# One hybrid decoder layer on Trainium2: tokens laid out by remainder modulo 4 within each tile of 128

## The chip, the cores and the metric

The kernel runs on one core of one Trainium2 chip. The metric is the device time of one launch in microseconds (us). A core has five engines, each with its own queue of instructions that it works through in order: TensorE (PE; PEld is its loading of weights), VectorE (DVE), ScalarE (ACT), GpSimd (POOL) and SyncE (SP), which here issues all transfers. Sixteen DMA engines carry them.

## The reference

One decoder layer over x of 1 x 1024 x 1024 (tokens x channels), float32:

```python
z = x @ w_in
u, rq, rk, rv, rg, aq, ak, av = split(z)
y_ssm = rms_norm(s5_mixer(u, ...), ssm_norm)        # 256 channels, state space model
y_ret = retention_mixer(rq, rk, rv, rg, ret_norm)   # 4 heads of 64, chunks of 128
y_att = rms_norm(dilated_attention_mixer(aq, ak, av), attn_norm)  # 8 heads of 64
h = concatenate([y_ssm, y_ret, y_att]) @ w_out
x = layer_norm(ALPHA * x + h, ln1_w, ln1_b)
h = square(relu(x @ mlp_w1)) @ mlp_w2
x = layer_norm(ALPHA * x + h, ln2_w, ln2_b)
```

The attention has three branches with (window, dilation) of (128, 1), (512, 4) and (2048, 16); a query of the second looks at keys 0, 4, 8, ... tokens back, so queries and keys fall into four classes by the token's remainder modulo 4.

## The kernel before

Products are done in pieces: an operand is split into a rounded part and a rest ("hi" and "lo", `H` and `L` in names), and three matmuls stand for one. Tokens are worked on in 8 tiles of 128 and in blocks of 512. A planner written in Python orders the work: the class `Clock` has a cost for each operation, transfers too, `Stream` starts coroutines by rank and blocks them at `when` and `flag`, and the order so found is the order of each engine's queue. On the chip the queues run in order, and what waits in one holds up all behind it.

The stages, in order of time: the projection by w_in (`dense`, its jobs' results taken from PSUM by `ev_u` and others); the state space model (`ssm_params`, `ssm`), retention, attention; the output projection in three parts (`out_b` with g = 0 and 1, `out_a`); layer norm 1; the MLP as products of sums of blocks (`up_sums`, `product`, `down`), layer norm 2 (`norm2`). The first are interleaved with one another.

The pieces that the change and the prediction speak of (all operations but matmuls and transposes are recorded with line 234, matmuls with line 394, transposes with 400):

- `ev_u` (L619): the part u of the projection, `uf`, is copied from PSUM by ScalarE in four pieces, and stored to `u_d` in DRAM in sixteen transfers, each `8x16x128` in the DRAM access pattern. `Tz` (L921) is loaded from `ker_d` by two transfers with an access pattern of 8 x 16 x 1024 on the DRAM side and 128 partitions on the other.
- `ssm` (L930): the gate, `og`, is the product of `glth` and `gT` on VectorE; then squares, scale and store to `mix_d`.
- `values` (L1218): V goes to DRAM (`v_d`) and comes back with its rows grouped in fours (`w`).
- `far` (L1251): scores of the near branch (y = 0) and the dilated branches (y = 1) of a head, 16 matmuls of 128x256 per head, `ps_f`; Q and K are read every fourth element for y = 1, and for y = 0 Q is cast once to an order by remainder, `by_r`.
- `mixed` (L1469): the sum of the hi and lo parts of the attention output, `mixp`, on VectorE.
- `load_x1` (L1616): once the last job of the projection is done ("last"), x is loaded into `X`, one transfer of 512 KB for each of the 8 token tiles; `out_b` for g = 0 adds products to them (`X<-X,pm`, in `add_b`, L1624).
- `out_b_load` and `out_b_split` (L1571, L1586) load W_out and the mix in pieces of 512 KB (`wraw`), cast them on ScalarE (`MB`) and find the rest on GpSimd; `out_b` for g = 1 has the matmuls `pm<-MB`.
- `down` (L2072): `rraw` is the MLP's inner result, read back from `r_d` in 512 KB pieces; `norm2` (L2045) stores the output `out` by `put`, a whole tile or parts of it, as the layer norm of a tile is done. The stores stand among the loads of `rraw` in SyncE's queue.

Of the kernel before, what the change touches and what calls it, by code (L numbers as in the profile page):

```python
# [13 lines left out]
F32R = mybir.dt.float32r  # L14
# [52 lines left out]
RET_LG = [math.log(1.0 - 2.0 ** (-5.0 - h)) for h in range(4)]  # L67


def shape_tables():  # L70

    qi = np.arange(128)[:, None]
    x = np.arange(512)[None, :]
    near = lambda d: (d <= 128).astype(np.float64)
    far = lambda d: ((d % 4 == 0) & (d <= 512)).astype(np.float64) + (d % 16 == 0)
    parts = []
    by_r = 4 * (qi % 32) + qi // 32
    for d, mult in ((384 + qi - x, lambda d: near(d) + far(d)), (128 + by_r - x[:, :256], near),
                    (4 * (128 + qi - x[:, :256]), far)):
        n = mult(d) * (d >= 0)  # L80
        lnc = np.log(np.where(n > 0, n, 1.0))
        parts.append(np.stack([np.where(n > 0, 2.0 ** -(h + 1.0) * d - lnc, 1e30) for h in range(NH)]))
    bias = np.concatenate(parts, 2)
    i = np.arange(128)
    df = i[None, :] - i[:, None]
    dm = np.stack([np.where(df >= 0, np.exp(np.maximum(df, 0) * lg), 0.0) for lg in RET_LG])
    dmat = dm.reshape(2, 2, 128, 128).transpose(2, 1, 0, 3)
    zeta = np.concatenate([np.repeat(np.exp((127.0 - i) * lg)[:, None], 64, 1) for lg in RET_LG], 1)
    xi = np.stack([np.concatenate([np.repeat(np.exp((i + 1.0) * RET_LG[2 * p + e])[None], 64, 0)
                                   for e in range(2)]) for p in range(2)], 1)  # L90
    f = lambda a: np.ascontiguousarray(a, dtype=np.float32)
    tabs = np.concatenate([zeta, xi.reshape(128, 256), dmat.reshape(128, 512)], 1)
    return {"c_bias": f(bias), "c_tabs": f(tabs)}
# [204 lines left out]
async def when(w, early=0.0):  # L298
    if isinstance(w, str):
        await ask(("flag", w))  # L300
    elif w:
        await ask(("data", w, early))
# [3 lines left out]
def trunk_kernel(ctx: ExitStack, tc: tile.TileContext, t_in, out):  # L306
# [43 lines left out]
    def free(*tiles):  # L350

        for t in tiles:
            if isinstance(t, (list, tuple)):
                free(*t)
            else:
                room = st_.room[tags.pop(t.tensor.name)]
                room[0] += 1
                room[1].append(clock.last[t.tensor.name])

    def U(shape, dt=F32, name="u", spare=2):  # L360
        return take(up, shape, dt, "u", NU, name, spare)

    async def Us(n, shape, dt=F32, name="u", spare=2):
        return [await U(shape, dt, name, spare) for _ in range(n)]
# [13 lines left out]
    def f(ap):  # L378
        return ap.bitcast(F32)
# [4 lines left out]
    async def stt(o, a, s, b, op0, op1):  # L384
        await dve.scalar_tensor_tensor(out=o, in0=a, scalar=s, in1=b, op0=op0, op1=op1)
# [233 lines left out]
    def ev_u(a):  # L619

        async def g(th, ps):
            if th == 0:
                T["uf", a] = await U([128, 8, 128], name="uf", spare=0)
            uf = T["uf", a]
            await act.copy(uf.rearrange("p j c -> p c j")[:, 64 * th:64 * th + 64], ps.rearrange("p (c j) -> p c j", j=8))
            free(ps)
            if th == 1:
                for j in range(8):
                    d = u_d[a][112 - 16 * j:128 - 16 * j]
                    await sp.dma_start(out=bass.AP(tensor=d.tensor, offset=d.offset, ap=[[128, 8], [1024, 16], [1, 128]]),  # L630
                                       in_=uf[:, j])
                free(T.pop(("uf", a)))
                T["UT", a] = await U([128, 8, 128], name="UT", spare=0)
                await sp.dma_start(out=T["UT", a], in_=u_d[a].rearrange("p (g c) -> p g c", g=8))
        return g
# [294 lines left out]
    async def ssm():  # L930
# [100 lines left out]
        for a in range(2):  # L1031
# [5 lines left out]
                await act.copy(gT[a][:, 4 * jq:4 * jq + 4], ps)  # L1037
                free(ps)
            free(gel[a])
        og = await Us(2, [128, 128, 8], name="og", spare=0)  # L1040
        sq = await Us(2, [128, S], name="sq", spare=0)
        jc = lambda v: v.rearrange("p j c -> p (j c)")
        for fo in range(2):
            for jq in range(2):
                q = slice(4 * jq, 4 * jq + 4)
                await when([gT[0][:, q], gT[1][:, q], wg])
                ps = await PS(name="ps_gl")
                for k in range(2):
                    await mm(ps, wg[:, k, fo * 128:(fo + 1) * 128], jc(gT[k][:, q]), k == 0, k == 1)
                th = await H([128, 4, 128], name="glth")  # L1050
                await act.activation(jc(th), ps, AF.Tanh, scale=0.25, bias=bglu[:, fo:fo + 1])
                await when([th])
                free(ps)
                await stt(og[fo].rearrange("p c j -> p j c")[:, q], th, 1.0, gT[fo][:, q], A_, M)
                free(th)
        free(wg, gT)
        for fo in range(2):
            o = og[fo].rearrange("p c j -> p (c j)")
            await when([o])
            await act.activation(sq[fo], o, AF.Square, scale=0.25)  # L1060
            await dve.tensor_scalar_mul(o, o, ssmw[:, fo:fo + 1])
            await sp.dma_start(out=mix_d[fo], in_=o)
            free(og[fo])
# [154 lines left out]
    async def values(p):  # L1218
# [18 lines left out]
        flag(f"V{p}")  # L1237
        for a in range(2):
            W = await U([128, 4, 2, 2, 64], F32R, "w")
            await sp.dma_start(out=f(W).rearrange("p r h s d -> p (r h s d)"),  # L1240
                               in_=v_d[p][512 * a:512 * a + 512].rearrange("(c r) v -> c (r v)", r=4))
            T["W", p].append(W)
        flag(f"W{p}")

# [6 lines left out]
    async def far(i_, h):  # L1251
# [7 lines left out]
            flag(f"stat{p}")  # L1259
        await when(f"stat{p}")  # L1260
        stat = T["stat", p]
        by_r = await U([128, 4, 4, 32], F32R, "by_r")
        await act.copy(by_r, Qs[:, 512:].rearrange("p (s a r) -> p s r a", s=4, r=4))
        P = await Us(2, [128, 4, 256], name="far")
        for y in (1, 0):
            s = P[y]
            for j in range(0, 4, 2):
                await when([Qs, KL, KH, bias] if y else [by_r])
                ps = await PS((128, 2, 256), "ps_f")
                qk = []  # L1270
                for a in (j, j + 1):
                    q = Qs[:, 512 + a:S:4] if y else by_r[:, a].rearrange("p r a -> p (r a)")
                    qk.append((q, slice(384 + 128 * a, 640 + 128 * a) if y == 0 else slice(a, S, 4)))
                for i, (q, k) in enumerate(qk):
                    await mm(ps[:, i], q, KH[:, k], i == 0, False)
                for i, (q, k) in enumerate(qk):
                    await mm(ps[:, i], q, KL[:, k], False, i == 1)
                for i in range(2):
                    await dve.tensor_tensor_reduce(
                        out=s[:, j + i], in0=ps[:, i], in1=bias[:, 512 + 256 * y:768 + 256 * y], scale=1.0,  # L1280
                        scalar=3e38, op0=ALU.add, op1=ALU.min, accum_out=stat[:, y, j + i, e, 0:1])
                free(ps)
        scored(h)
        free(by_r)
        for y in (1, 0):
            for j in range(4):
                await act.activation(P[y][:, j], P[y][:, j], AF.Exp, scale=-1.0, bias=stat[:, y, j, e, 0:1],
# [181 lines left out]
    async def mixed(h, po, c0, n, ms, classes=1):  # L1469
# [7 lines left out]
        mix = T["mix", p]  # L1477
        vl = await H([64, n], name="vl")
        await act.copy(vl, po[64:128, :n])
        by_r = lambda v: v.rearrange("p (r a) -> p r a", r=classes)  # L1480
        await tt(dve, mix[b, c].rearrange("p (a r) -> p r a", r=classes), by_r(po[:64, :n]), by_r(vl), A_)
        free(vl, po)
        if not counted(("mix", p, c0), 2):
            return
# [111 lines left out]
    async def out_b(g):  # L1596
# [16 lines left out]
        else:  # L1613
            flag("outb")

    async def load_x1():  # L1616
        await when("last")
        X1 = big("A", [128, 8, D], "X1", F32)
        x1.extend(X1[:, t] for t in range(8))
        for t in range(8):  # L1620
            await sp.dma_start(out=x1[t], in_=x_d[t * 128:(t + 1) * 128, :])
            flag(f"xl{t}")

    async def add_b(t, dh, g, ps, v):  # L1624
# [219 lines left out]
    async def up_sums():  # L1844
        for q in range(NQ):
            await when(f"ul{q}")
            wa, wb = raws["u", q]
            s1 = await U([128, 2, 512], name="ws", spare=3)
            s3 = await U([128, 2, 512], name="ws", spare=3)
            raws["us", q] = s1, s3  # L1850
            await tt(dve, s1[:, 0], wb[:, 0], wb[:, 1], A_)
            await tt(dve, s1[:, 1], s1[:, 0], wa[:, 0], SUB)
            await tt(dve, s3[:, 0], wa[:, 0], wb[:, 0], SUB)
            await tt(dve, s3[:, 1], wa[:, 1], s1[:, 1], SUB)
            flag(f"us{q}")
# [188 lines left out]

    async def norm2(t):  # L2045
        def put(c):
            return sp.dma_start(out=out_d[t * 128:(t + 1) * 128, c], in_=x1[t][:, c])

        await when("ln2")
        await layer_norm(t, lnw["ln2_w"], lnw["ln2_b"], put)  # L2050
# [84 lines left out]
def host_arrays(inputs):  # L2135

    src = {n: np.ascontiguousarray(inputs[n]) for n in _INS}
    kp = lambda w: w.reshape(w.shape[0] // 128, 128, -1).transpose(1, 0, 2)
    src["x_t"] = np.ascontiguousarray(inputs["x"][0].reshape(8, 128, 8, 128).transpose(0, 3, 2, 1))
    w = inputs["w_in"][0]  # L2140
    units = []
    for kind, c0 in JOBS:
# [37 lines left out]
```

## Time and profile before

| | |
|---|---|
| median of 3 runs | 1168.99 us (1168.92 to 1169.17) |
| the profiled execution, its own time | 1170.03 us |
| its span | 1168.3 us |
| TensorE busy | 1122.4 us, 96% |
| VectorE, ScalarE, GpSimd busy | 70%, 46%, 20% |
| granted clock of TensorE, mean | 0.991 of full |
| bytes moved by DMA | 175.4 MB |

A profile is one execution. The span runs from the first to the last instruction of the core; times in it are counted from its start. "Busy" is the time in which at least one instruction of an engine ran; matmuls overlap, so that their durations sum to more than the time that they take. Where an engine was idle, the profile names the instruction or transfer whose end released it.

### The profile page before, as it was taken

The numbers are of one execution on the slowest core, as the hardware profiler recorded it, in microseconds if no ns is written. First come the engines' busy times: TensorE is split into PE (matmuls) and PEld (weight loads), VectorE is DVE, ScalarE is ACT, GpSimd is POOL, SyncE is SP. The second block draws the span as 40 slices with busy tenths as digits, with TensorE's granted clock in tenths as the row PEclk, the third lists the DMA queues.
The fourth block names the chain that finished last, engine by engine and source line by source line (L and its number), as shares of the span: only waits on it lengthen the run. The fifth ranks groups of instructions, "written<-read, shape, count | busy, mean of one in ns | idle before, by whom it ended". The sixth has DMA issues, their size and how long they took to land.

```text
span 1168.3 us, 15903 instructions
## 1 busy us (share of the span) xinstructions
PE 1122.4 (96%) x5825; PEld 950.5 (81%) x5825; DVE 814.3 (70%) x1665; ACT 532.3 (46%) x941; POOL 239.4 (20%) x183
## 2 busy tenths in 40 slices
PE   8999999899999989999999999999999999999996
PEld 7889888778888777887778888888788888888875
DVE  5986567676563688899776766667457785675865
ACT  5121322676756657336445454545444343442530
POOL 1232316635164533466000000000000000000104
PEclk9999999899999999999999999999999999999989
DMA  8000421520151624034263444434598667767521
GB/s 320 19 1 31 137 74 49 194 92 19 37 182 64 226 90 153 33 122 163 98 219 143 173 150 155 156 142 154 180 350 333 199 202 248 270 223 263 191 81 72
DMA packets 65133, 175.36 MB, mean 150 GB/s; under 512 B 7064, under 2 KB 16800, under 8 KB 65056
## 3 DMA queue, kind: packets, MB, share of 16 engines
q1 hardware_dynamic: 65056, 174.35, 42.6%
q8 instruction: 46, 0.75, 0.3%
q14 instruction: 31, 0.25, 0.1%
HBM read 127.42 MB, written 46.91 MB: 149 GB/s over the span
## 4 chain that ended last, share of the span: by engine, by line
PE 44%; DVE 4%; DMA 1%; issue 1%; ACT 1%; SPq 0%; DVEq 0%; POOL 0%
PE ps L394 27%; PE pm L394 17%; DVE dol L234 1%; DVE X L234 1%; DMA wraw<-in_mlp_w_units 1%; DMA rraw<-r_d 0%; DVE rs L234 0%; DMA K<-in_mlp_w_units 0%; DVE wop L234 0%; DVE SQ L234 0%; DVE ws L234 0%; ACT rb L234 0%; ACT X L234 0%; ACT doh L234 0%; DVE rb L234 0%
## 5 line engine op out<-in xcount | busy, mean ns | idle before, releaser
L234 POOL TENSOR_TENSOR lnr<-lnr,nhalf 128x1 f32<-128x1 f32 x16 | 10.9, 684 | 592.8 <-DVE lnmv L234 530.1
L394 PE MATMUL ps<-xoh,wop 128*128 128x512 f32 x384 | 123.7, 390 | 1.8 <-DVE u L234 1.8
L394 PE MATMUL pm<-doh 128*128 128x512 f32 x256 | 100.9, 394 | 3.0 <-DVE X L234 3.0
L234 ACT CAST doh<-rraw 128x1024 fp32r<-128x1024 f32 x56 | 58.7, 1049 | 93.2 <-DMA rraw<-r_d 73.2
L394 PE MATMUL pm<-dol,doh 128*128 128x512 f32 x256 | 100.8, 394 | 0.0
L394 PE MATMUL pm<-doh,dol 128*128 128x512 f32 x256 | 100.7, 393 | 0.0
L394 PE MATMUL pm<-XOB,wop 128*128 128x512 f32 x384 | 95.2, 393 | 0.2 <-DVE wop L234 0.2
L394 PE MATMUL ps<-XOA,wop 128*128 128x512 f32 x384 | 91.2, 390 | 3.6 <-DVE wop L234 3.6
L234 DVE TENSOR_TENSOR dol<-rraw,doh 128x1024 fp32r<-128x1024 f32 x56 | 68.4, 1221 | 33.0 <-ACT doh L234 33.0
L394 PE MATMUL pm<-XA,whi 128*128 128x512 f32 x224 | 89.3, 399 | 0.0
L394 PE MATMUL pm<-XA,wlo 128*128 128x512 f32 x224 | 88.6, 396 | 0.0
L394 PE MATMUL pm<-XB,whi 128*128 128x512 f32 x224 | 88.5, 395 | 0.0
L394 PEld LDWEIGHTS ps<-XOA,wop 128*128 128x128 f32 x384 | 71.9, 188 | 19.7 <-DVE wop L234 4.8
L394 PEld LDWEIGHTS ps<-xoh,wop 128*128 128x128 f32 x384 | 72.1, 188 | 17.4 <-DVE u L234 2.2
L234 ACT ACTIVATE rb<-rb 128x512 f32<-128x512 f32 x64 | 40.5, 633 | 98.6 <-DVE rb L234 97.6
L394 PEld LDWEIGHTS pm<-XOB,wop 128*128 128x128 f32 x384 | 71.0, 188 | 14.6 <-DVE wop L234 0.6
L234 POOL TENSOR_TENSOR wlo<-wraw,whi 128x1024 fp32r<-128x1024 f32 x24 | 58.3, 2440 | 104.2 <-ACT whi L234 83.9
L394 PE MATMUL ps<-xol,wop 128*128 128x512 f32 x192 | 74.7, 389 | 0.0
L394 PE MATMUL ps<-doh 128*128 128x512 f32 x192 | 74.7, 389 | 0.0
L394 PE MATMUL ps<-dol,doh 128*128 128x512 f32 x192 | 74.7, 389 | 0.0
L394 PE MATMUL ps<-doh,dol 128*128 128x512 f32 x192 | 74.7, 389 | 0.0
L394 PEld LDWEIGHTS pm<-doh 128*128 128x128 f32 x256 | 48.6, 190 | 14.3 <-issue 2.8
(286 smaller groups left out, 2802.9 us busy)
## 6 DMA issues: line engine op xcount, KB each, us to landing
wraw<-in_mlp_w_units SPq DMA_DIRECT2D x92, 512.0 KB
rraw<-r_d SPq DMA_DIRECT2D x56, 512.0 KB
r_d<-rs SPq DMA_DIRECT2D x32, 512.0 KB
wraw<-in_w_in_units SPq DMA_DIRECT2D x20, 512.0 KB
v_d<-v SPq DMA_DIRECT2D x8, 512.0 KB
w<-v_d SPq DMA_DIRECT2D x8, 512.0 KB
abias<-in_c_bias SPq DMA_DIRECT2D x8, 512.0 KB
wraw<-in_w_out SPq DMA_DIRECT2D x8, 512.0 KB
```

The source lines that it names most:

```text
L234: fn(*a, **kw)
L394: nc.tensor.matmul(ps, a, b, start=start, stop=stop, skip_group_check=open_)
```

## The change

The tokens of each tile of 128 are laid out by remainder: place p of a tile holds token 4 (p mod 32) + p / 32, so a class is a run of 32 places in a tile. Tables of biases and decays (`shape_tables`) and the transposed x (`host_arrays`) follow on the host. On the chip: `ev_u` copies each piece in two halves, eight copies with every second element read; `ssm` writes `og` in sixteen products; `values` reads back in 32 transfers for 8; `far` scores the near part first, casts the dilated part's Q to `Qr`, and reads Q as contiguous and K as runs of 32; `mixed` adds in runs of 32; the loads of `X` and the stores of `out` go through a new helper, `rows`, whose DRAM side has 4 blocks of 32 rows each, 4 rows apart. `up_sums` waits for a flag of the quarter before besides.

```diff
+BY_R = 4 * (np.arange(128) % 32) + np.arange(128) // 32
...
@@ ev_u
-            await act.copy(uf.rearrange("p j c -> p c j")[:, 64 * th:64 * th + 64], ps.rearrange("p (c j) -> p c j", j=8))
+            for b in range(2):
+                await act.copy(uf[:, 4 * b:4 * b + 4, 64 * th:64 * th + 64].rearrange("p r (t a) -> p t r a", t=4),
+                               ps.rearrange("p (t r a b) -> p t r a b", t=4, r=4, b=2)[:, :, :, :, b])
@@ ssm
-                await stt(og[fo].rearrange("p c j -> p j c")[:, q], th, 1.0, gT[fo][:, q], A_, M)
+                for r in range(4):
+                    by_t = lambda v: v.rearrange("p (t a) -> p t a", t=8)
+                    await stt(og[fo][:, :, r, :, jq], by_t(th[:, r]), 1.0, by_t(gT[fo][:, 4 * jq + r]), A_, M)
@@ values
-            await sp.dma_start(out=f(W).rearrange("p r h s d -> p (r h s d)"),
-                               in_=v_d[p][512 * a:512 * a + 512].rearrange("(c r) v -> c (r v)", r=4))
+            for t in range(4):
+                await sp.dma_start(out=f(W)[32 * t:32 * t + 32].rearrange("p r h s d -> p r (h s d)"),
+                                   in_=v_d[p][512 * a + 128 * t:512 * a + 128 * t + 128].rearrange("(r c) v -> c r v", r=4))
@@ far
-        by_r = await U([128, 4, 4, 32], F32R, "by_r")
-        await act.copy(by_r, Qs[:, 512:].rearrange("p (s a r) -> p s r a", s=4, r=4))
+        by_r = lambda v: v.rearrange("p (t r a) -> p r t a", r=4, a=32)
+        Qr = await U([128, 4, 128], F32R, "Qr")
+        await act.copy(Qr.rearrange("p r (t a) -> p r t a", t=4), by_r(Qs[:, 512:]))
...
-        for y in (1, 0):
+        for y in (0, 1):
...
-                    q = Qs[:, 512 + a:S:4] if y else by_r[:, a].rearrange("p r a -> p (r a)")
-                    qk.append((q, slice(384 + 128 * a, 640 + 128 * a) if y == 0 else slice(a, S, 4)))
+                    if y:
+                        qk.append((Qr[:, a], *(by_r(v)[:, a] for v in (KH, KL))))
+                    else:
+                        k = slice(384 + 128 * a, 640 + 128 * a)
+                        qk.append((Qs[:, 512 + 128 * a:640 + 128 * a], KH[:, k], KL[:, k]))
@@ mixed
-        await tt(dve, mix[b, c].rearrange("p (a r) -> p r a", r=classes), by_r(po[:64, :n]), by_r(vl), A_)
+            by_r = lambda v: v.rearrange("p (r s a) -> p r s a", r=4, a=32)
+            await tt(dve, mix[b, c].rearrange("p (s r a) -> p r s a", r=4, a=32), by_r(po[:64, :n]), by_r(vl), A_)
@@ load_x1 and norm2
+    def rows(d, t, c):
+        v = d[t * 128:(t + 1) * 128, c]
+        return bass.AP(tensor=v.tensor, offset=v.offset, ap=[[D, 4], [4 * D, 32], [1, c.stop - c.start]])
...
-            await sp.dma_start(out=x1[t], in_=x_d[t * 128:(t + 1) * 128, :])
+            await sp.dma_start(out=x1[t], in_=rows(x_d, t, slice(0, D)))
...
-            return sp.dma_start(out=out_d[t * 128:(t + 1) * 128, c], in_=x1[t][:, c])
+            return sp.dma_start(out=rows(out_d, t, c), in_=x1[t][:, c])
@@ up_sums
+            if q:
+                await when(f"uw{q - 1}.5")
```

The planner then finds a somewhat other order where attention is interleaved with the rest. On SyncE around the loads of `X`, before (rows by engine, `out<-in` and shape; the line is that of the helper):

```order
L234 DMA mix_d<-mixp 128x1024
L234 DMA wraw<-in_w_in_units 128x1024
L234 DMA abias<-in_c_bias 128x1024 x2
L234 DMA X_3982<-in_x 128x1024 x8
L234 DMA abias<-in_c_bias 128x1024
L234 DMA wraw<-in_w_out 128x1024
L234 DMA wraw<-mix_d 128x1024
```

and with the change:

```order
L239 DMA w<-v_d_80 32x4x256 x8
L239 DMA mix_d<-mixp 128x1024
L239 DMA X_3983<-in_x 128x1x1024 x8
L239 DMA abias<-in_c_bias 128x1024
L239 DMA wraw<-in_w_out 128x1024
L239 DMA wraw<-mix_d 128x1024
```

The read-back of V, now eight transfers, has moved to just ahead of the loads of `X`; behind them the same three follow. For the loads order prints the shape of the side in the core's memory; it was `128x1x1024` for `Tz<-ker_d` too, in both kernels.

On SyncE where the last layer norm begins, with the change:

```order
L239 DMA out<-X_8152 4x32x1024
L239 DMA rraw<-r_d_2_102 128x1024
L239 DMA out<-X_8152 4x32x1024
L239 DMA rraw<-r_d_3_106 128x1024
L239 DMA rraw<-r_d_4_110 128x1024
...
L239 DMA out<-X_8152 4x32x1024
L239 DMA out<-X_8152 4x32x512 x5
L239 DMA out<-X_8152 4x32x256 x2
```

The rows stand where they stood; the stores of `out` were `128x1024`, `128x512` and `128x256` before.

On TensorE, from the first `pm<-MB` on (`ident,s` is a transpose, `pt` a transposed block of attention weights, `w` and `v` its values), before:

```order
L394 MATMUL pm<-MB 128x512 x2
L394 MATMUL pm<-whi,wlo 128x512
L394 MATMUL pm<-whi 128x512
L394 MATMUL pm<-MB 128x512
L394 MATMUL pm<-wlo,whi 128x512
...
L394 MATMUL ps_f<-KH,Qs 128x256 x2
L394 MATMUL ps_f<-KL,Qs 128x256 x2
L394 MATMUL ps_f<-KH,by_r 128x256 x2
L394 MATMUL ps_f<-KL,by_r 128x256 x2
L394 MATMUL ps_f<-KH,by_r 128x256 x2
L394 MATMUL ps_f<-KL,by_r 128x256 x2
L394 MATMUL pm<-MB 128x512 x12
```

and with the change:

```order
L399 MATMUL pm<-MB 128x512 x2
L399 MATMUL pm<-wlo,whi 128x512
L399 MATMUL pm<-whi,wlo 128x512
L405 MATMUL ps_pt<-ident,s 128x128 x3
L399 MATMUL ps_o<-pt,w 128x128 x3
...
L399 MATMUL ps_f<-KH,Qs 128x256 x2
L399 MATMUL ps_f<-KL,Qs 128x256 x2
L399 MATMUL ps_f<-KH,Qr 128x256 x2
L399 MATMUL ps_f<-KL,Qr 128x256 x2
L399 MATMUL pm<-MB 128x512
```

Before, `ps_f<-KH,Qs` are the dilated matmuls and `by_r` the near ones; with the change `Qs` are the near and `Qr` the dilated ones, and they follow. Up to about 234 us and from about 535 us on, TensorE's rows are the same as before.

## Rows read from the trace of the kernel before

**Rows 1.** Busy time by stretch: window, length, PE, PEld, DVE, ACT, POOL, clock, DMA share, GB/s
```profile
230.00:377.00 147.00, 141.44 (x860) 123.98 (x860) 88.39 (x243) 100.50 (x246) 62.44 (x48) 1.00 0.23 79
```
**Rows 2.** Groups by form, TensorE's scores in `far`: busy, mean ns of one | idle before
```profile
L394 PE MATMUL ps_f<-KH,Qs 128*128 128x256 f32 x32 | 11.2, 442 | 0.0
L394 PE MATMUL ps_f<-KH,by_r 128*128 128x256 f32 x32 | 7.7, 321 | 1.4 <-DVE stat L234 1.4
```
**Rows 3.** Timeline of TensorE, one head's scores: start, length, instruction, count
```profile
408.77 0.66 PE L394 MATMUL ps_f<-KL,Qs 128*128 128x256 f32 x2
409.24 0.67 PE L394 MATMUL ps_f<-KH,Qs 128*128 128x256 f32 x2
...
410.46 0.40 PE L394 MATMUL ps_f<-KL,by_r 128*128 128x256 f32 x2
410.70 0.40 PE L394 MATMUL ps_f<-KH,by_r 128*128 128x256 f32 x2
```
**Rows 4.** Timeline of SyncE's queue around the loads of X
```profile
377.41 3.74 SPq L234 DMA_DIRECT2D X<-in_x  x8
...
394.11 0.33 SPq L234 DMA_DIRECT2D wraw<-in_w_out  x1
```
**Rows 5.** Busy time by stretch, columns as in rows 1: the loads of Tz, of X
```profile
121.50:129.50 8.00, 8.00 (x38) 6.60 (x37) 4.03 (x21) 1.43 (x2) 2.94 (x2) 1.00 0.51 131
...
378.00:389.00 11.00, 10.50 (x52) 8.67 (x50) 6.78 (x29) 8.61 (x38) 1.03 (x6) 1.00 0.96 379
```
**Rows 6.** Timeline of SyncE's queue, 120 to 155 us
```profile
120.06 1.83 SPq L234 DMA_DIRECT2D Tz<-ker_d  x2
...
148.40 0.38 SPq L234 DMA_DIRECT2D mix_d<-yo  x1
149.35 4.88 SPq L234 DMA_DIRECT2D u_d<-uf  x8
```
**Rows 7.** DMA packets, 149.2 to 155.9 us
```profile
DMA packets 1362, 0.81 MB, mean 121 GB/s; under 512 B 80, under 2 KB 1360, under 8 KB 1360
```
**Rows 8.** DMA packets and issues, 1150 to 1168 us
```profile
DMA packets 1153, 2.11 MB, mean 117 GB/s; under 512 B 128, under 2 KB 384, under 8 KB 1152
...
out<-X SPq DMA_DIRECT2D x5, 256.0 KB
```
**Rows 9.** Timelines of ScalarE and TensorE: start, length, instruction, idle before and its releaser
```profile
397.59 1.05 ACT L234 CAST MB<-wraw 128x1024 fp32r<-128x1024 f32 x1 [0.78 <-DMA wraw<-in_w_out]
...
403.35 0.61 PE L394 MATMUL pm<-MB 128*128 128x512 f32 x2
...
415.48 4.15 PE L394 MATMUL pm<-MB 128*128 128x512 f32 x10 [2.34 <-POOL MB L234]
```
**Rows 10.** Timeline of SyncE's queue, 1100 us to the end
```profile
1103.20 0.34 SPq L234 DMA_DIRECT2D out<-X  x1
...
1106.61 0.34 SPq L234 DMA_DIRECT2D out<-X  x1
...
1150.32 15.65 SPq L234 DMA_DIRECT2D out<-X  x8
```
**Rows 11.** The chain of waits: start, length, what
```profile
1107.04 4.58 DMA rraw<-r_d
...
1115.19 4.96 PE pm L394 x13
```
**Rows 12.** Groups by form, ScalarE and VectorE, columns as in rows 2
```profile
L234 ACT COPY vl<-ps_o 64x256 f32<-64x256 f32 x16 | 5.8, 369 | 7.7 <-PE ps_o L394 7.4
L234 ACT COPY uf<-pm 128x512 f32<-128x512 f32 x4 | 4.3, 1073 | 10.8 <-PE pm L394 10.8
...
L234 DVE SCALAR_TENSOR_TENSOR og<-glth,gT 128x512 f32<-128x512 f32 x4 | 4.4, 1102 | 3.3 <-ACT glth L234 3.3
L234 DVE SCALAR_TENSOR_TENSOR gel<-gt,ps_y 128x128 f32<-128x128 f32 x16 | 3.4, 282 | 1.8 <-ACT gt L234 1.8
```
**Rows 13.** Busy time by stretch, columns as in rows 1
```profile
207.50:214.40 6.90, 5.57 (x26) 5.57 (x27) 1.22 (x3) 3.30 (x4) 2.59 (x2) 0.51 0.64 217
```

More of the change, by code (lines that the diff above doesn't have):

```diff
@@ L73, in shape_tables @@
     x = np.arange(512)[None, :]
+    tok = 128 * (x // 128) + BY_R[x % 128]
     near = lambda d: (d <= 128).astype(np.float64)
@@ L76, in shape_tables @@
     parts = []
-    by_r = 4 * (qi % 32) + qi // 32
-    for d, mult in ((384 + qi - x, lambda d: near(d) + far(d)), (128 + by_r - x[:, :256], near),
+    by_r = BY_R[:, None]
+    for d, mult in ((384 + by_r - tok, lambda d: near(d) + far(d)), (128 + by_r - tok[:, :256], near),
                     (4 * (128 + qi - x[:, :256]), far)):
@@ L83, in shape_tables @@
     bias = np.concatenate(parts, 2)
-    i = np.arange(128)
+    i = BY_R
     df = i[None, :] - i[:, None]
@@ L1039, in ssm @@
             free(gel[a])
-        og = await Us(2, [128, 128, 8], name="og", spare=0)
+        og = await Us(2, [128, 8, 4, 16, 2], name="og", spare=0)
         sq = await Us(2, [128, S], name="sq", spare=0)
@@ L1057, in ssm @@
         for fo in range(2):
-            o = og[fo].rearrange("p c j -> p (c j)")
+            o = og[fo].rearrange("p t r a b -> p (t r a b)")
             await when([o])
@@ L1261, in far @@
         stat = T["stat", p]
-        by_r = await U([128, 4, 4, 32], F32R, "by_r")
-        await act.copy(by_r, Qs[:, 512:].rearrange("p (s a r) -> p s r a", s=4, r=4))
+        by_r = lambda v: v.rearrange("p (t r a) -> p r t a", r=4, a=32)
+        Qr = await U([128, 4, 128], F32R, "Qr")
+        await act.copy(Qr.rearrange("p r (t a) -> p r t a", t=4), by_r(Qs[:, 512:]))
         P = await Us(2, [128, 4, 256], name="far")
-        for y in (1, 0):
+        for y in (0, 1):
             s = P[y]
             for j in range(0, 4, 2):
-                await when([Qs, KL, KH, bias] if y else [by_r])
+                await when([Qr, KL, KH, bias] if y else [Qs, KL, KH, bias])
                 ps = await PS((128, 2, 256), "ps_f")
@@ L1271, in far @@
                 for a in (j, j + 1):
-                    q = Qs[:, 512 + a:S:4] if y else by_r[:, a].rearrange("p r a -> p (r a)")
-                    qk.append((q, slice(384 + 128 * a, 640 + 128 * a) if y == 0 else slice(a, S, 4)))
[L1274 to L1277, printed above, removed]
+                    if y:
[3 more added lines that the diff above has]
+                        qk.append((Qs[:, 512 + 128 * a:640 + 128 * a], KH[:, k], KL[:, k]))
+                for i, (q, k, _) in enumerate(qk):
+                    await mm(ps[:, i], q, k, i == 0, False)
+                for i, (q, _, k) in enumerate(qk):
+                    await mm(ps[:, i], q, k, False, i == 1)
                 for i in range(2):
@@ L1283, in far @@
         scored(h)
-        free(by_r)
+        free(Qr)
         for y in (1, 0):
@@ L1479, in mixed @@
         await act.copy(vl, po[64:128, :n])
-        by_r = lambda v: v.rearrange("p (r a) -> p r a", r=classes)
-        await tt(dve, mix[b, c].rearrange("p (a r) -> p r a", r=classes), by_r(po[:64, :n]), by_r(vl), A_)
+        if classes == 1:
+            await tt(dve, mix[b, c], po[:64, :n], vl, A_)
+        else:
+            by_r = lambda v: v.rearrange("p (r s a) -> p r s a", r=4, a=32)
+            await tt(dve, mix[b, c].rearrange("p (s r a) -> p r s a", r=4, a=32), by_r(po[:64, :n]), by_r(vl), A_)
         free(vl, po)
@@ L2138, in host_arrays @@
     kp = lambda w: w.reshape(w.shape[0] // 128, 128, -1).transpose(1, 0, 2)
-    src["x_t"] = np.ascontiguousarray(inputs["x"][0].reshape(8, 128, 8, 128).transpose(0, 3, 2, 1))
+    src["x_t"] = np.ascontiguousarray(inputs["x"][0].reshape(8, 128, 8, 128)[:, BY_R].transpose(0, 3, 2, 1))
     w = inputs["w_in"][0]
```

## The prediction

> **What bounds the kernel now.** I read the busy time by stretch first, then the groups of instructions, then the queue of SyncE, the DMA counts and the chain of waits. In the stretch in which the attention heads and the last projection jobs run, TensorE is busy 141.4 of 147.0 us [rows 1], so a shorter matmul there shortens the stretch almost one for one, and so it is in most of the program. Two places are ruled by transfers instead. Behind the last projection job SyncE issues the eight loads of `X` at 377.4 [rows 4]; the first half of W_out, issued at 394.1 behind them in the same queue, is waited for by ScalarE's cast at 397.6, and that cast feeds the matmuls `pm<-MB` that begin at 403.4 and again, after a wait of 2.3 us, at 415.5 [rows 9]. Near the end the chain of waits runs through one load, `rraw`, 4.58 us from 1107.04, and on from it to the matmuls at 1115.2 [rows 11]; that load is issued behind an output store at 1106.6 [rows 10].
>
> **How many DMA engines a transfer gets.** This decides the case, so I looked for transfers of before whose access pattern does not begin with 128 rows. `Tz<-ker_d` is a load with 8 rows outermost on the DRAM side, `u_d<-uf` a store with 8. Two `Tz` loads of 512 KB are issued at 120.1 [rows 6]; from 121.5 to 129.5 the DMA engines are busy for a share of 0.51 and move 131 GB/s, whereas the loads of `X` of before run at 0.96 and 379 GB/s [rows 5]. Half of the sixteen engines did all the work: 4.0 us for 512 KB, and the two loads shared the same half, one behind the other, or the share would have been nearer 1. The packet counts say the same of the store. Eight output stores leave 128 packets below 512 B, 16 each [rows 8]; the window with eight `u_d` stores and the tail of one `mix_d<-yo` store issued just ahead of them [rows 6] has 80, that is 8 × 8 + 16, and not 8 × 16 + 16 = 144 [rows 7]. So an outermost count of 8 gave 8 engines, in both directions.
>
> The helper `rows` puts a dimension of 4 outermost on the DRAM side of every load of `X` and every output store. By the same reading each runs on 4 engines. No row of before has a 4; that is the inference on which the forecast hangs. [...]
>
> **Price of a 512 KB load on 4 engines.** Full rate: 379 GB/s over 0.96 of 16 engines is 24.7 GB/s for one, so 524 KB on four takes 5.3 us. At the rate of `Tz`, 131 GB/s over 0.51 of 16, 16.1 GB/s for one: 8.0 us. I take 8.0: `Tz` is the nearest row, a load from DRAM into 128 partitions on a part of the engines with 4 KB runs, and it is the only such row. The ends are 5.3 and 8.0. [...]
>
> **The change, part by part.**
> 1. `far`: 64 matmuls of the dilated branch read Q and K every fourth element (442 ns mean against 321 for the contiguous ones of the same size [rows 2]). They overlap, so I take the distance of starts: two strided ones 0.47 us, two contiguous ones 0.24 [rows 3], 0.116 us less for each, if runs of 32 read as fast as contiguous ones. That is 7.4 us of TensorE: 5.6 for the 48 that stand ahead of the loads of `X`, 1.9 for the 16 behind the first `pm<-MB`. If runs of 32 cost as much as the stride, 0.
> 2. Loads of `X`: issued at 377.4 − 5.6 = 371.8, first packet a microsecond later as now (issue 377.4 [rows 4], traffic from 378 on [rows 5]), eight times 8.0: done at 436.8, where 16 engines needed 11 us. In the order of SyncE the `abias` load and the W_out load still stand behind them. Both use all engines, so four shares of each wait: 2 × 1.3 us (524 KB at 395 GB/s) and 1.0 to be noticed: 440.4 in place of 397.6 for the cast [rows 9], **+42.8 us** (which holds the 5.6 of point 1). At 5.3 us a load it is 372.8 + 42.4 + 3.6 = 418.8, +21.2. Nothing covers it: VectorE's sums `X<-X,pm` wait for these loads one token tile at a time and stand in order ahead of the attention's work, so TensorE runs dry too. Up to 4.8 us may come back, since after so long a wait GpSimd and ScalarE have no backlog and the 12.1 us from 403.4 to 415.5 [rows 9] hold more waiting than matmuls need; up to 3 us may be lost to the clock, which was granted at 0.51 for 6.9 us behind an earlier stall [rows 13]. I let these two cancel.
> 3. Work behind the first `pm<-MB`: 16 faster dilated matmuls, −1.9; and one block of attention (`high`), 34 small transposes and matmuls, now stands ahead of it in TensorE's order, at most 34 × 0.12 = 4.1, at least 0, I take −3. Together **−4.9**.
> 4. Output stores in the middle of the last layer norm: 5.3 us on four engines for 1.3 on sixteen. The store runs the other way, and `u_d` shows no row that is slow, so full rate is taken; the other end is 8.0. The store issued at 1103.2 starts at 1104.2 and ends at 1109.5; the `rraw` behind it takes 1.3 (1110.8), the store of 1106.6 ends at 1116.1, the `rraw` of the chain at 1117.4. With 1.3 for each store the same sum ends at 1110.2, and the trace's 1111.6 less a microsecond to be noticed is near it [rows 10, 11]. **+7.2 us**; TensorE waits for it, as the chain shows.
> 5. The tail: eight stores issued from 1150.3 on [rows 10], 512 + 5 × 256 + 2 × 128 KB, 2.1 MB at 4 × 24.7 GB/s: 21.2 us, with a microsecond at each end 1173.5, against a span of 1168.3: **+5.2 us**.
> 6. `ev_u`: four copies of 1073 ns [rows 12] become eight of half the size that read every second word of PSUM. Bounds: as quick as a 64x256 copy, 369 ns [rows 12], or half of 1073 and a fixed part, some 640: 3.0 to 5.1 us for 4.3. I take no change; ScalarE has idle time there, and if it had not it would be at most 0.8. [...]
> 7. `ssm`: four products of 1102 ns become sixteen of 128x128; the nearest row is 282 [rows 12], 4.5 us for 4.4. Bounds 0.2 to 0.42 each, −1.2 to +2.3 on VectorE, and the stores of `og` that follow are wanted only tens of microseconds later: 0.
> 8. `values`: 24 more issues on SyncE, 0.47 each by the loads of `X` [rows 4], in four places, under 3 us in each. The rows come in order 32 deep, so all engines work. Behind them stand weight loads and, last, the loads of `X`, which wait for the jobs anyway: 0; without that cover 2.8 us once.
> 9. The smaller cast of Q, the mix on VectorE in runs of 32, the wait in `up_sums`: the first two take time off engines that are not waited for. The third changes no order on TensorE (from the MLP on its rows are the same as before): 0. Should it cost, it is a sum on VectorE that comes one product later, some 1 us.
>
> **Sum**: 42.8 − 4.9 + 7.2 + 5.2 = +50.3 on the profiled execution of 1170.0 (span 1168.3): 1220.3. The median of the runs is 1.0 below that execution, so 1219.
>
> **Rivals.**
> - *The four-fold outermost dimension does not confine the transfer* (it is merged with the 32, or the 128 rows of the other side decide). Then loads and stores take what they take now, and of the sum only point 1 is left: the 7.4 us of the dilated matmuls, 1161.6: faster. For it: the SBUF side of the loads still has 128 rows. Against it: `Tz` stands in the order with the same 128 rows on that side and got 8 engines. The point is whether the share of the DMA engines in the load is above 0.5.
> - *Four engines at full rate*: +21.2 in place of +42.8, 1197.5. For it: a stretch of `u_d` packets shows no slowing. Against: `Tz`.
> - *Stores as slow as `Tz`* besides slow loads: 8.0 for 5.3 in point 4 (+5.4), 32 us for 21.2 in point 5 (+10.8): 1235.
> - *Hidden anyway*: the loads could start earlier than I think and lie beside attention work. They are issued as soon as the last job's buffers are free, and the sums that need them come 4 us later now; there is work for a few microseconds only, so this gives 1166 to 1172 at very best.
>
> **How the numbers follow.** Forecast 0.55, full-rate loads 0.18, slow stores too 0.14, sixteen engines 0.09, hidden or partly spread 0.04. Predicted time 1219. The range takes in the full-rate case less the 4.8 of point 2 (1192.7) and a little for the unpriced ends, and the slow-store case with the clock's 3 us: 1190 to 1238; left out are the sixteen-engine and the hidden case and some tails. A measurement of this kernel tells about 0.2%, 2.3 us, from no change. Faster is the sixteen-engine case and a part of the hidden one, 0.10; same 0.02; slower 0.88.
>
> **What would show it.** After the change the share of the DMA engines in the loads of `X` should read 0.25, for some 64 us; the eight output stores should leave 32 packets below 512 B in place of 128; ScalarE's first cast of `MB` should wait for `wraw<-in_w_out` until about 440; the dilated `ps_f` matmuls should take as long as the others; the eight stores of the tail should keep the DMA engines at a share near 0.25 for about 21 us without a gap. A share of 0.9 or more in the loads refutes it at once; a load of 5.3 us puts it at the second rival.

## The result

The changed kernel takes 1219.25 us (median of 6 runs, 1216.8 to 1222.4), the kernel before 1169.08 in the same comparison: a ratio of 1.0431, 95% interval 1.0409 to 1.0453. The forecast was 1219. The time was met; the terms that make it up were not: the loads cost less than forecast, the stores and a stretch forecast at nothing cost more.

The lag of one and the same matmul can be read in two places. The 192 products that end the output projection stand in the same order in both kernels, and behind about 558 us of the kernel before TensorE's rows are the same altogether. (They are so only from there on, not from 535 us as said above: between 505 and 558 us transposes stand at other places among the products.) The profiled execution of the changed kernel has a span of 1220.3 us, 52.0 more than before.

| place | start before | start after | lag |
|---|---|---|---|
| a product of the output projection | 505.17 | 525.60 | 20.4 |
| behind the first products of the MLP | 563.17 | 587.66 | 24.5 |
| an early part of the MLP, 60 us on | 623.61 | 649.64 | 26.0 |
| ahead of the last layer norm | 1101.80 | 1127.25 | 25.4 |
| behind its first stores | 1130.89 | 1173.33 | 42.4 |
| last matmul | 1159.00 | 1201.43 | 42.4 |
| end of the span | 1168.3 | 1220.3 | 52.0 |

So 20.4 us come from the first half, 5.6 from the beginning of the MLP (of which 0.6 come back later), 17.0 from the stores in the middle of the last layer norm, 9.6 from the tail.

**The loads of `X`.** Busy time by stretch while they run, changed kernel (window, length, the engines' busy time and counts, clock, share of the DMA engines, GB/s):

```profile
380.00:400.00 20.00, 15.38 (x57) 12.22 (x58) 11.88 (x38) 10.29 (x39) 2.36 (x10) 0.77 0.26 105
```

The share is a quarter, where it was 0.96 [rows 5]: four engines. But they move 105 GB/s, 26 for each, no less than an engine moved in the plain loads of before (379 GB/s at 0.96 of sixteen, 24.7 [rows 5]), not the 16 of `Tz`. SyncE's queue (start, length, instruction):

```profile
371.51 24.90 SPq L239 DMA_DIRECT2D X<-in_x  x8
396.53 4.68 SPq L239 DMA_DIRECT2D abias<-in_c_bias  x1
401.31 0.38 SPq L239 DMA_DIRECT2D wraw<-in_w_out  x1
```

The loads go out at 371.5, as forecast (371.8), but their eight issues now take 24.9 us, against 3.74 [rows 4]: SyncE itself stood still, and W_out is issued at 401.3. The sums on VectorE and the first cast of `MB` on ScalarE (start, length, instruction, idle before and its releaser):

```profile
379.97 0.69 DVE L239 SCALAR_TENSOR_TENSOR X<-X,pm 128x512 f32<-128x512 f32 x1 [4.64 <-DMA X<-in_x]
...
384.95 0.69 DVE L239 SCALAR_TENSOR_TENSOR X<-X,pm 128x512 f32<-128x512 f32 x1 [2.13 <-DMA X<-in_x]
...
390.36 0.69 DVE L239 SCALAR_TENSOR_TENSOR X<-X,pm 128x512 f32<-128x512 f32 x1 [1.98 <-DMA X<-in_x]
...
395.25 0.69 DVE L239 SCALAR_TENSOR_TENSOR X<-X,pm 128x512 f32<-128x512 f32 x1 [2.19 <-DMA X<-in_x]
```

```profile
421.37 1.04 ACT L239 CAST MB<-wraw 128x1024 fp32r<-128x1024 f32 x1 [17.47 <-DMA wraw<-in_w_out]
```

From the first to the fourth of these sums a token tile lands every 5.1 us and VectorE waits for it, and the cast comes at 421.4 instead of 397.6 [rows 9]: +23.8.

**The stores.** The chain of waits in the last layer norm, and TensorE there:

```profile
1115.73 11.20 DMA rraw<-r_d
...
1139.47 13.74 DMA rraw<-r_d
...
1156.79 45.05 PE pm L399 x186
```

```profile
1151.22 0.77 PE L399 MATMUL pm<-doh 128*128 128x512 f32 x1 [16.34 <-DVE X L239]
1156.79 0.79 PE L399 MATMUL pm<-doh 128*128 128x512 f32 x1 [2.66 <-DVE X L239]
```

The load of `rraw` that took 4.58 us [rows 11] takes 13.74, another one ahead of it 11.20, each behind an output store. ScalarE's casts of these two, before and then with the change:

```profile
1094.07 1.05 ACT L234 CAST doh<-rraw 128x1024 fp32r<-128x1024 f32 x1 [0.67 <-DMA rraw<-r_d]
...
1111.64 1.04 ACT L234 CAST doh<-rraw 128x1024 fp32r<-128x1024 f32 x1 [2.00 <-DMA rraw<-r_d]
```

```profile
1127.01 1.05 ACT L239 CAST doh<-rraw 128x1024 fp32r<-128x1024 f32 x1 [7.08 <-DMA rraw<-r_d]
...
1153.23 1.04 ACT L239 CAST doh<-rraw 128x1024 fp32r<-128x1024 f32 x1 [4.21 <-DMA rraw<-r_d]
```

Beyond the lag of 25.4 that was there, the first comes 7.5 us late, the second 16.2. TensorE stands for 16.3 us and then works at a granted clock of 0.50 from 1150 to 1162 us, which adds 0.8:

```profile
1150.00:1162.00 12.00, 8.11 (x18) 5.95 (x19) 8.77 (x13) 7.67 (x8) 0.00 (x0) 0.50 0.12 48
```

In the tail:

```profile
1194.00:1199.00 5.00, 5.00 (x24) 4.14 (x23) 3.42 (x8) 0.00 (x0) 3.47 (x3) 1.00 0.25 52
1199.00:1203.00 4.00, 2.82 (x13) 2.01 (x11) 1.92 (x3) 0.00 (x0) 2.56 (x2) 1.00 0.24 95
1203.00:1213.00 10.00, 0.00 (x0) 0.00 (x0) 4.84 (x9) 0.00 (x0) 2.22 (x2) 0.68 0.26 101
```

DMA packets from 1192 us to the end, then from 1199.0 to 1200.5 us (with packets, MB and share of 16 engines):

```profile
DMA packets 1058, 2.12 MB, mean 73 GB/s; under 512 B 32, under 2 KB 288, under 8 KB 1056
...
DMA packets 30, 0.12 MB, mean 82 GB/s; under 512 B 0, under 2 KB 0, under 8 KB 30
q1 hardware_dynamic: 30, 0.12, 20.6%
```

32 packets below 512 B for eight stores, 4 each, where there were 128 [rows 8]. The 512 KB store, 4 KB a row, begins at 52 GB/s on its quarter of the engines, 13 for each, half of the 26 that they reach in the loads. The next 1.5 us still move rows of 4 KB (30 packets, 0.12 MB) at 82 GB/s on 0.206 of 16 engines, 25 for each, and behind that the rate is 95 to 101. So the slow part is the beginning of the store, and not the length of its rows.

**The beginning of the MLP.** TensorE's waits there, with the change:

```profile
536.65 0.66 PE L405 MATMUL ps_x<-ident,x 128*128 128x128 f32 x4 [1.74 <-POOL x L239]
...
564.97 0.33 PE L405 MATMUL ps_x<-ident,x 128*128 128x128 f32 x1 [1.19 <-POOL x L239]
...
583.40 3.97 PE L399 MATMUL ps<-XOA,wop 128*128 128x512 f32 x15 [1.82 <-ACT wop L239]
```

and the longest of before:

```profile
529.85 0.66 PE L400 MATMUL ps_x<-ident,x 128*128 128x128 f32 x4 [0.78 <-POOL x L234]
```

With the change TensorE waits here twice for `x`, which GpSimd writes, and once for a cast on ScalarE, 5.0 us in all with a shorter wait, against 1.4 before; that is most of the 4.1 by which the lag grows to 24.5. The other 1.5 us, near 610 us, are the clock: granted 0.72 from 608 to 614 us, 1.00 in the same stretch of the kernel before. They do not belong to the change: e8, in the old order, has 0.72 and the same 1.5 us there, and e12, in the new order, has 1.00 and no loss.

**The rest.** Groups by form, changed kernel:

```profile
L399 PE MATMUL ps_f<-KH,Qr 128*128 128x256 f32 x32 | 8.4, 341 | 0.3 <-DVE stat L239 0.3
L399 PE MATMUL ps_f<-KH,Qs 128*128 128x256 f32 x32 | 7.2, 307 | 0.0
...
L239 ACT COPY uf<-pm 128x256 f32<-128x256 f32 x8 | 2.6, 378 | 10.7 <-PE pm L399 10.7
...
L239 DVE SCALAR_TENSOR_TENSOR og<-glth,gT 128x128 f32<-128x128 f32 x16 | 3.6, 289 | 4.7 <-ACT glth L239 4.7
```

Runs of 32 read nearly as fast as contiguous rows (341 against 307 ns; the stride took 442 [rows 2]). The copies of `uf`, which read every second word of PSUM, take 378 ns, nearly as little as contiguous ones of as many columns (369 [rows 12]).

### The profile page after: what moved, and what is told of

It is laid out like the page before. It is cut to its first block, busy times and chain, and to the rows that moved or that the text cites. A ratio compares the mean times of both kernels' runs of the same rounds, so it can differ in the third digit from the quotient of the medians.

```text
span 1220.3 us, 15969 instructions
## 1 busy us (share of the span) xinstructions
PE 1129.1 (93%) x5825; PEld 954.5 (78%) x5825; DVE 810.7 (66%) x1677; ACT 523.8 (43%) x945; POOL 242.1 (20%) x183
## 4 chain that ended last, share of the span: by engine, by line
PE 69%; DVE 12%; DMA 8%; issue 4%; ACT 3%; POOL 1%; SPq 1%; DVEq 0%; ACTq 0%; POOLq 0%
PE pm L399 34%; PE ps L399 26%; PE ps_o L399 2%; DVE par L239 2%; DMA rraw<-r_d 2%; DMA wraw<-in_w_out 2%; DMA X<-in_x 2%; DVE X L239 1%; PE ps_pt L405 1%; DVE dol L239 1%; PE ps_f L399 1%; SPq L239 1%; ACT far L239 1%; PE ps_s L399 1%; DVE pt L239 1%
```

## The experiments

All comparisons are with the kernel before, run on the same chip.

**e1 and e2: loads alone, stores alone over 32 rows.** For e1, and alike for the stores in e2 (the planner is told of one transfer, so that no other engine's rows move):

```diff
-            await sp.dma_start(out=x1[t], in_=rows(x_d, t, slice(0, D)))
+            await sp.spread(x1[t], rows(x_d, t, slice(0, D)),
+                            [(x1[t][32 * r:32 * r + 32], row1(x_d, t, r, slice(0, D))) for r in range(4)])
```

> The changed kernel with each load of X issued as four transfers of 32 rows, a remainder class each, so that 32 rows stand outermost; the rows of all other engines stay as they are. Theory: the four-engine loads cost the 20.4 us by which TensorE's rows lag at the output projection, and the 5.4 us it had gained before them comes back to the fore, so the time falls by 25 us or so, to 1194 us, and the share of the DMA engines in the loads reads over 0.9. Rival, that the new order of attention costs it: not below 1213 us.

> The changed kernel with each output store issued as four transfers of 32 rows. Theory: the 17.0 us lost in the middle of the last layer norm and the 9.6 us of the tail are both the stores' four engines, so the time falls by 24 to 27 us, to 1192 to 1195 us, and TensorE's wait of 16.3 us there goes back to some 2.5 us. Rival, that rows 4 apart in DRAM write slowly however they are spread: 1210 us or more.

e1: 1198.7 us (4 runs, 1193.2 to 1200.1), ratio 1.0247 [1.0217, 1.0277]. e2: 1202.4, ratio 1.0286 [1.0263, 1.0309]. Both took off less than expected, 20 and 17 us. In e2 TensorE's wait in the last layer norm falls to

```profile
1142.28 0.77 PE L405 MATMUL pm<-doh 128*128 128x512 f32 x1 [5.06 <-DVE X L245]
```

so it is the stores that the `rraw` loads stand behind; neither rival holds.

**e3: both.**

> The changed kernel with loads and stores both issued as four transfers of 32 rows. Theory: nothing is left of the loss, and the dilated matmuls' gain of 7.4 us shows: 1161 to 1164 us. Rival, that the 5.5 us which TensorE loses between 514 and 600 us in the changed kernel belong to the wait added in up_sums or to the order: 1166 to 1168 us. A second rival, that 32 partitions at a time fill the engines badly: 1170 us or more.

1180.0 us, ratio 1.0094 [1.0073, 1.0115]: 39 us of the 50 are gone, 11 remain. It is the second rival's number, but by another way than the rival says. The loads:

```profile
369.00:382.00 13.00, 11.63 (x60) 9.24 (x59) 9.03 (x37) 10.15 (x43) 1.60 (x8) 1.00 1.01 246
```

All DMA engines are busy (share 1.01), but with 32 rows at a time they move 246 GB/s, not 379 [rows 5]. That costs nothing that shows: at the output projection TensorE is 4.1 us ahead of the kernel before (6.2 in e1, with the same loads). What makes the profiled execution's span 10.5 us longer in the end comes behind that: 5.5 us at the beginning of the MLP (see e12), 1.6 by the clock there, 3.5 in the middle of the last layer norm and 4.1 in the tail.

**e4: `far` alone**, put into the kernel before.

> The kernel before with the changed far alone (near part first, Q of the dilated part cast to runs, K read in runs of 32); the tokens' layout stays, so the dilated scores are taken of other tokens than they should be. Theory: the strided reads alone cost TensorE 7.4 us, so 1161 to 1163 us. Rival, that the stretch is held by other engines as much as by TensorE: 1166 to 1169 us.

1169.6 us (10 runs), ratio 1.0015 [0.9997, 1.0033]: the rival. The gain is there when the loads of `X` begin (issued at 371.41, 6.0 earlier than before), and TensorE's 2400th instruction starts 7.6 us earlier; at the end of the output projection 0.3 us are left. In between TensorE waits for the attention's own steps (the second of these waits was there before, with 1.40 us), and then the clock is granted at 0.50 for a while, where it was 1.00:

```profile
414.85 0.62 PE L394 MATMUL ps_o<-pt,v 128*128 128x256 f32 x3 [2.47 <-DVE pt L234]
...
450.28 0.44 PE L400 MATMUL ps_pt<-ident,s 128*128 128x128 f32 x2 [1.54 <-DVE s L234]
...
455.48 0.90 PE L394 MATMUL ps_o<-pt,v 128*128 128x256 f32 x3 [1.46 <-DVE pt L234]
```

```profile
455.00:460.00 5.00, 4.39 (x20) 3.99 (x20) 3.32 (x8) 2.37 (x6) 1.64 (x2) 0.50 0.01 2
```

**e5: plain rows.** Loads and stores as before, all else as in the changed kernel.

> The changed kernel with the loads of X and the stores of the output as they were before, 128 rows in the order of DRAM, so that residual and output rows are not those of the layout; the order of all engines is that of the changed kernel. The kernel with both spread over 32 rows still took 11 us more than the one before. Theory: what is left there is the price of four times as many transfers of 32 rows (8.4 us at the loads, 3.5 in the middle of the last layer norm, 4.1 in the tail), so 1164 to 1166 us here. Rival: it is the order of the work, the wait in up_sums foremost, so 1173 to 1178 us.

1170.75 us (10 runs), ratio 1.0013 [0.9999, 1.0027]: between the two, and equal to the kernel before. So all that the changed kernel loses lies in how `X` and `out` are moved, and the layout's other parts bring nothing in sum. The 9 us between e3 and e5 are the price of transfers of 32 rows, and by TensorE's lag most of it is paid at the stores: 3.5 us in the last layer norm and 4.1 in the tail in e3, 0.6 and 0.0 in e5. At the output projection e5 is 1.8 us ahead of before, e3 4.1. So the theory's 8.4 us at the loads is not there.

**e6, e7: the loads alone, the stores alone, in the kernel before.** One line each, as in the change.

> The kernel before with the loads of X alone through the helper rows, all other rows of all engines as before; the residual's tokens are in the wrong places. Theory: the loads on four engines cost by themselves what they cost in the changed kernel against its spread form, 24.5 us: 1191 to 1196 us. Rival, that in the old order W_out is hidden better or worse: 1185 or less, or 1200 or more.

> The kernel before with the output stores alone through the helper rows; the output's tokens are in the wrong places. Theory: 17.0 us in the middle of the last layer norm and 9.6 us in the tail, as the changed kernel showed: 1194 to 1197 us. Rival, that the middle was long only since the layer norm began in another state: 1185 us or less.

e6: 1196.9 us, 1.0236 [1.0208, 1.0264]. e7: 1196.0, 1.0227 [1.0203, 1.0251]. e7 lies in the theory's range, e6 just above its own: 27 and 26 us, together 54, where the change lost 50. In e7 the two `rraw` loads of the chain take what they take in the changed kernel:

```profile
1092.15 11.32 DMA rraw<-r_d
...
1116.01 13.73 DMA rraw<-r_d
```

**e8 and e12: the wait in `up_sums`**, alone in the kernel before, and from the third quarter on only in e5.

> The kernel before with the wait added in up_sums alone. Theory: the sums that come later cost the 5.5 us that TensorE's rows lag from 514 to 600 us in the changed kernel: 1173 to 1175 us. Rival, no cost, as forecast: 1168 to 1170 us.

> The kernel of e5 (plain rows, order of the changed kernel, residual and output rows not those of the layout) with the added wait of up_sums from the third quarter on only, not for the second. In all kernels with the changed order TensorE's rows lag by 3 to 6 us more after the MLP's first quarter, in those with the old order by 0 to 1.6. Theory: in this order the wait for the second quarter's sums costs it: 1165 to 1167 us. Rival: it is the rest of the order: 1169 to 1172 us.

e8: 1168.9 us (10 runs), 0.9994 [0.9983, 1.0005]: no cost. e12: 1172.7 (7 runs), 1.003 [1.0015, 1.0044], a little above the rival's range, with the loss in the MLP's beginning still there. Both rivals hold in kind: it is not the wait. From 505 to 563 us of the kernel before, TensorE loses 4.1 to 6.0 us in every kernel with its new order there (the changed one, e1, e2, e3, e5, e11, and e12 with 6.0), and nothing (−0.1 to 0.0) in every kernel with the old one (e4, e6 to e10). Which row of the new order makes it is open.

**e9 and e10: other counts of blocks**, in the kernel before, loads and stores alike:

```diff
+        return bass.AP(tensor=v.tensor, offset=v.offset, ap=[[D, 16], [16 * D, 8], [1, c.stop - c.start]])
```

> The kernel before with loads of X and output stores through a helper of the same form as rows, with 16 blocks of 8 rows, 16 rows apart, in place of 4 blocks of 32; the residual's and the output's tokens are in the wrong places. Theory: it is the outermost count alone, so nothing is lost: 1168 to 1171 us, and the share of the DMA engines in the loads is above 0.9. Rival: scattered rows in DRAM are slow by themselves, so 1185 us or more.

> The same with 8 blocks of 16 rows, 8 rows apart. Theory: eight engines; the loads take 20 us for 10 and half of that is hidden as the last tiles are wanted later, the stores in the middle take 2.7 us for 1.3 each and the tail 10 us of traffic, most of it under the work: 1174 to 1184 us, share near 0.5 in the loads. Rival, four engines here too, or a loss in proportion: 1195 us or more.

e9: 1176.3 us, 1.0073 [1.0048, 1.0097], between theory and rival; e10: 1199.1, 1.0266 [1.0244, 1.0287], a time in the rival's range, though not by four engines. The loads, first of e9, then of e10:

```profile
379.00:388.00 9.00, 9.00 (x47) 7.79 (x46) 5.55 (x23) 6.92 (x30) 0.00 (x0) 1.00 0.94 228
```

```profile
378.00:389.00 11.00, 9.84 (x48) 7.71 (x46) 5.33 (x25) 7.60 (x33) 0.00 (x0) 1.00 0.51 130
```

The shares are as expected, 0.94 and 0.51: with the 0.26 of the changed kernel, the share of the engines in these loads went with the outermost count, 16, 8 and 4. The speed of one engine goes another way: 24.7 GB/s in plain loads, 15 with 16 blocks, 16 with 8, 26 with 4. So eight blocks load by a quarter faster than four (130 GB/s against 105) and not twice as fast; at the output projection TensorE lags 16 us in e10, 30 in e6.

**e11: the layout with wide transfers.** Loads of 32 rows by four tiles, tail stores on two queues.

> The changed kernel with the loads of X as eight transfers of 32 rows by four tiles, one remainder class each (32 outermost, as many issues as before), and the stores as four transfers of 32 rows, in the tail every second one issued by ScalarE's queue in place of SyncE's. Theory: the 9.3 us by which the spread form stands above the plain rows are issues on SyncE, 32 for 8, so 1171 to 1175 us. Rival, that 32 partitions at a time use the DMA engines badly: 1179 us or more.

1186.2 us, 1.0152 [1.0131, 1.0173], slower than e3. The rival's number:

```profile
370.00:388.00 18.00, 9.68 (x46) 8.00 (x45) 6.42 (x32) 7.88 (x35) 0.00 (x0) 0.81 1.03 212
```

Fewer issues, but 212 GB/s, and no tile is whole before its four classes are: TensorE lags 6.2 us at the output projection, where e3 is 4.1 ahead. As e3 moves hardly more (246 GB/s) and loses nothing there, the late tiles are the likelier reason; no run parts the two. In the tail, with the second queue, 2.1 us are lost, against 4.1 in e3. The best version of the layout with rows in their places is e3, 11 us behind the kernel before; no kernel here beats that one.

## Why the prediction was right, and where its steps were wrong

- **Four engines (right).** The reading of `Tz` and `u_d` held for 4: a share of 0.26 in the loads, 4 packets below 512 B a store. In the loads of `X` the shares at 4, 8 and 16 blocks were 0.26, 0.51 and 0.94 (the changed kernel, e10, e9).
- **8.0 us a load (wrong).** Point 2 took `Tz`'s rate as the nearest row; measured 5.1. The cast moved by 23.8 us, not 42.8; the second rival had 21.2. Why it came 2.6 above that is open; W_out was issued only at 401.3, while the loads still ran. What failed is the step "it is the only such row": `Tz`'s rate goes with eight blocks, as e10 shows on `X` itself (16 GB/s), and does not carry over to four (26).
- **Work behind the first `pm<-MB` (−4.9).** The lag falls from 23.8 at the cast to 20.4 at the output projection, so −3.4.
- **The stores (wrong).** Point 4 had +7.2, measured 17.0; point 5 had +5.2, measured 9.6. Point 4's sum began with the store of 1103.2. Two more stores stand ahead of it in the same layer norm, and the `rraw` behind the first of them comes 7.5 us late by itself; the store of 1103.2 then goes out at 1135.4, 6.8 us later than the lag of 25.4 has it. The pair that was counted adds 8.7, the clock 0.8. And 5.3 us a store was too little: "`u_d` shows no row that is slow" did not carry over. In the tail the 512 KB store ran its first five microseconds at 52 GB/s, half of the 105 that four engines moved in the loads. e7 shows the same 16 and 9 us and the same slow beginning (54 GB/s, then 93) with nothing else changed. Why a store begins slowly is open.
- **The beginning of the MLP (missed).** 5.6 us where 0 was forecast. 4.1 are TensorE's waits in the new order, 1.5 a stretch of lower clock: 0.72 from 608 to 614 us in the changed kernel and in e8 with the old order, 1.00 there in the kernel before and in e12 with the new one. Point 9 took TensorE's rows as the same "from the MLP on"; they differ up to about 558 us of the kernel before, and every kernel with the new rows there loses 4.1 to 6.0. e8 and e12 clear the wait.
- **The dilated matmuls (right in size, wrong in effect).** The loads go out 5.9 us earlier, 6.0 in e4, where 5.6 was forecast. But the forecast counted them as won; e4 shows that the attention's end gives them back (7.6 us ahead at the 2400th instruction, 0.3 at the output projection), and e5 that most of it is given back in the new order too (6.1 and 1.8). As the loads were late anyway, the sum did not feel it.
- **`uf`, `og`, `values`, the casts (right): nothing.** They were not tried alone; e5, which has all of them, equals the kernel before. `uf` came near its lower bound, 378 ns for 369.

The sum: 23.8 − 3.4 + 5.6 − 0.6 + 17.0 + 9.6 = 52.0, where the forecast had 42.8 − 4.9 + 7.2 + 5.2 = 50.3. The loads were over by 19.0, the rest under by 20.7. The direction and the four engines were foreseen; that the time agrees to 0.3 us is chance.

## What to carry to other kernels

Ahead of any change of layout, write out the access pattern of each large transfer with both sides' dimensions: here one helper with 4 as the outermost count cost 50 us, and VectorE, which had not waited for the loads of `X` before, stood for them 2.0 to 4.6 us ahead of each of the first four tiles once a tile took 5.1 us. Read the price from a transfer with the same outermost count, since the speed of one engine did not follow from its neighbours' (26 GB/s with 4 blocks, 16 with 8, 15 with 16). In a queue, begin the sum with the first transfer that is slowed, not with the one on which the chain of waits stands today. A gain on the busiest engine counts only if the stretch behind it can take it up (in e4, 7.6 us became 0.3): run that part alone before it goes into the sum.

## What the runs showed of the hardware that was not expected

- The eight issues of the loads of `X` held SyncE's queue for 24.9 us with 4 blocks (the changed kernel), 9.78 with 8 (e10), 5.14 with 16 (e9) and 3.74 with plain rows [rows 4].
- At shares of 0.94 to 1.03 of the sixteen DMA engines, the loads of `X` ran at 379 GB/s by plain rows into 128 partitions [rows 5], at 228 with 16 blocks (e9), and at 246 and 212 in transfers of 32 partitions (e3, e11); the four engines of the changed kernel ran at 26 GB/s each. Why is open. At 228 and 246 GB/s (e9, e3) TensorE lost no more than 2 us by the output projection.
- On the same four engines and with the same 4 KB rows, the loads ran at 105 GB/s, and the first store of the tail at 52 for five microseconds (13 an engine), then at 25 an engine; e7 has 54 and then 93 GB/s. Why is open.
